# First pair of gate and up tiles as eight plain block products, and the second norm's roots in two steps

## The chip, the cores and the metric

The kernel runs on one core of one Trainium2 chip. The metric is the device time of one execution in microseconds (us), the median over several runs. Five engines work side by side and are ordered by semaphores: TensorE (PE, with its weight loads shown as PEld), VectorE (DVE), ScalarE (ACT), GpSimd (POOL) and SyncE (SP), which issues the DMAs.

## The reference

One layer of a decoder for 1024 prompt tokens and 8 x 8 sample tokens. What matters here is its second half; the input projection, the convolution heads and the attention come before it:

```python
x = x + jnp.concatenate([a, o], axis=-1) @ w_out          # output projection, residual
h = rms_norm(x, norm_ffn_g)                               # second norm, over 1024 features
g_full = jnp.concatenate([ffn_past, h @ w_ffn_gate], axis=1)
g = depthwise_conv_valid(g_full, ffn_conv_w, ffn_conv_b)  # width 3, along the tokens
x = x + (jax.nn.silu(g) * (h @ w_ffn_up)) @ w_ffn_down
```

with `rms_norm(x, g) = x * rsqrt(mean(x * x) + 1e-6) * g`. D_MODEL is 1024 and D_FF is 2816; everything is float32.

## The kernel before

Activations lie with features on the partitions: `x2` is 8 tiles (KT) of 128 features by N = 1088 tokens (1024 + 64). The tokens are taken in two halves of HN = 544. Each float32 operand is split into a high part, which ScalarE rounds to the fast matmul type, and a low part, the difference, which VectorE makes for activations (`split`) and POOL for weights (`weight_parts`). A product is then three matmuls: high by high, high by low, low by high. One block product is 4 feature tiles x 2 pieces of 272 tokens x 3 = 24 matmuls of 128x272.

The stage of this study ("F" in the code) does three things one after the other.

- `out_half(0)` and `out_half(1)`: the last part of the output projection, for the first and the second half of the tokens. For each of the 8 feature tiles it multiplies 12 matmuls, adds the result into `x2` (VectorE), stores the tile to DRAM (`x2d`, a DMA on SP's queue), squares it (ScalarE) and adds the square to a running sum (VectorE). 
- `rstd`: the norm's factor of one half. Matmuls with a column of ones add the sum up over the partitions and put the tokens on the partitions (L191), VectorE and ScalarE form 1/sqrt on a small tile (L193 to L206), and transposes (L213) and a copy spread it over all partitions again. For the first half this stands inside `out_half(1)`, behind its fourth tile (`norm_first`, m == 3); for the second half behind its last tile.
- `ffn_pair(j)` for j = 0 to 10: the gate's and up's tiles j and j + 11 (HF = 11). Two feature tiles of output, two halves of the input features and two halves of the tokens make a 2 x 2 block product, formed in Winograd's way with seven block products in place of eight (`products`). It needs sums and differences of token blocks (b11, b21 and b22 are plain blocks; t1 to t4 are combined) and of weight blocks (s1 to s4, made by `blocks_of_both` with four VectorE sums, L918 to L921).

The first pair differs: PE has nothing else to do while the blocks are being made. `products(..., first=True)` takes the seven products in another order (b11, b21, b22, t3, t2, t1, t4). `first_blocks` makes the b11 and b21 blocks of the first token half: four scales (`scale`, multiplying x by the norm's factor and weight), then four splits.

The order of the instructions on each engine comes from a scheduler, which takes them by a model of their times; `tc.issue_after(i)` adds an edge that keeps what is inside behind instruction i. Accumulators lie in four pairs of PSUM banks (`pair`: px, py, pz, pv).

## Time and profile before

| | |
|---|---|
| median of 3 runs | 1429.69 us (1428.96 to 1431.0) |
| profiled execution | 1432.72 us, span 1430.9 us |
| mean granted TensorE clock | 0.975 |
| busy, share of the span | PE 94%, PEld 89%, DVE 60%, ACT 36%, POOL 30% |
| stage F | 603.6 to about 1135 us of the span |
| instructions in stage F on PE | 192 matmuls of the output projection, 3696 of gate and up |

Times in the profile count from the start of the span. A row of the timeline gives start, duration, engine, line, operation, out<-in, count and, in brackets, the idle time ahead of it and what ended it. Busy shares are averages over stages with different limits. The matmuls overlap on PE, so a row of a matmul lasts longer than the distance to the next.

### The profile page before, as it was taken

The numbers are of one execution on the slowest core, as the hardware profiler recorded it, in microseconds if no ns is written. First come the engines' busy times: TensorE is split into PE (matmuls) and PEld (weight loads), VectorE is DVE, ScalarE is ACT, GpSimd is POOL, SyncE is SP. The second block draws the span as 40 slices with busy tenths as digits, with TensorE's granted clock in tenths as the row PEclk, the third lists the DMA queues.
The fourth block names the chain that finished last, engine by engine and source line by source line (L and its number), as shares of the span: only waits on it lengthen the run. The fifth ranks groups of instructions, "written<-read, shape, count | busy, mean of one in ns | idle before, by whom it ended". The sixth has DMA issues, their size and how long they took to land.

```text
span 1430.9 us, 24745 instructions
## 1 busy us (share of the span) xinstructions
PE 1350.0 (94%) x10011; PEld 1280.5 (89%) x10011; DVE 861.0 (60%) x1649; ACT 514.3 (36%) x982; POOL 431.5 (30%) x303
## 2 busy tenths in 40 slices
PE   6999999999999998976999999999999999999995
PEld 6988889999977777876899999999999889999995
DVE  7398595566574665679756566655656642423146
ACT  5312211457565564345333323333332321212033
POOL 3221111110000115231454445545445211224124
PEclk9999999999999998987999999999999999999998
DMA  7246676746699887340022122122212571414003
GB/s 271 54 139 245 226 255 206 206 141 179 180 276 226 243 228 225 112 162 8 30 91 91 65 87 91 52 70 91 91 62 91 167 291 45 139 48 131 11 9 118
DMA packets 84882, 195.16 MB, mean 136 GB/s; under 512 B 12576, under 2 KB 46752, under 8 KB 84768
## 3 DMA queue, kind: packets, MB, share of 16 engines
q1 hardware_dynamic: 84768, 193.57, 42.8%
q8 instruction: 79, 1.29, 0.4%
q14 instruction: 35, 0.29, 0.1%
HBM read 145.03 MB, written 48.52 MB: 135 GB/s over the span
## 4 chain that ended last, share of the span: by engine, by line
PE 76%; DVE 12%; DMA 6%; issue 2%; POOL 1%; ACT 1%; SPq 1%; POOLq 0%; ACTq 0%; DVEq 0%
PE g L174 9%; PE g L172 9%; PE g L173 9%; PE py L840 4%; PE py L842 4%; PE py L843 4%; DVE cacc L333 4%; PE o L666 3%; PE s L581 3%; PE pz L843 3%; PE pz L842 3%; PE pz L840 3%; PE px L843 3%; PE px L840 3%; PE px L842 3%; PE t L649 3%
## 5 line engine op out<-in xcount | busy, mean ns | idle before, releaser
L148 POOL TENSOR_TENSOR wl<-wr,wh 128x768 fp32r<-128x768 f32 (+2 forms) x61 | 117.1, 1921 | 464.7 <-PE g L174 391.8
L172 PE MATMUL g<-xh,wh 128*128 128x384 f32 (+1 forms) x472 | 158.6, 336 | 0.0
L173 PE MATMUL g<-xl,wh 128*128 128x384 f32 (+1 forms) x472 | 157.4, 333 | 0.0
L174 PE MATMUL g<-xh,wl 128*128 128x384 f32 (+1 forms) x472 | 157.2, 333 | 0.0
L172 PE MATMUL g<-ah,wh 128*128 128x384 f32 (+1 forms) x432 | 141.6, 333 | 5.0 <-ACT ah L1135 3.3
L173 PE MATMUL g<-al,wh 128*128 128x384 f32 (+1 forms) x432 | 143.0, 331 | 1.7 <-DVE al L1136 1.7
L174 PE MATMUL g<-ah,wl 128*128 128x384 f32 (+1 forms) x432 | 142.7, 331 | 0.7 <-POOL wl L148 0.7
L146 ACT ACTIVATE wh<-wr 128x768 fp32r<-128x768 f32 (+2 forms) x62 | 52.0, 838 | 241.0 <-PE g L174 177.5
L903 POOL TENSOR_TENSOR s<-wr,s 128x1024 fp32r<-128x1024 f32 x44 | 107.5, 2444 | 89.7 <-ACT s L902 47.9
L1158 DVE TENSOR_TENSOR x<-g,x 128x384 f32<-128x384 f32 (+1 forms) x72 | 38.0, 534 | 137.4 <-PE g L174 137.2
L622 ACT ACTIVATE y<-y,m 128x128 f32<-128x128 f32 (+1 forms) x192 | 88.4, 463 | 32.9 <-DVE m L610 32.9
L174 PEld LDWEIGHTS g<-xh,wl 128*128 128x128 f32 x472 | 90.0, 191 | 2.3 <-issue 2.1
L585 DVE CUSTOM_DVE_ANT_0 y<-s,pmk 128x128 f32<-128x128 f32 (+1 forms) x192 | 63.9, 378 | 45.8 <-PE s L581 36.9
L172 PEld LDWEIGHTS g<-xh,wh 128*128 128x128 f32 x472 | 90.1, 191 | 1.4 <-issue 1.2
L173 PEld LDWEIGHTS g<-xl,wh 128*128 128x128 f32 x472 | 90.0, 191 | 1.1 <-issue 1.0
L172 PEld LDWEIGHTS g<-ah,wh 128*128 128x128 f32 x432 | 82.0, 191 | 5.9 <-ACT ah L1135 3.6
L173 PEld LDWEIGHTS g<-al,wh 128*128 128x128 f32 x432 | 81.9, 190 | 2.0 <-DVE al L1136 2.0
L174 PEld LDWEIGHTS g<-ah,wl 128*128 128x128 f32 x432 | 81.8, 189 | 1.0 <-POOL wl L148 1.0
L333 DVE SCALAR_TENSOR_TENSOR cacc<-gp,prm,cacc 128x1024 f32<-128x1024 f32 x60 | 80.1, 1335 | 0.1
L1087 DVE SCALAR_TENSOR_TENSOR fc<-gb,prm,fc 128x1104 f32<-128x1104 f32 x44 | 79.0, 1813 | 2.0 <-ACT fc L1085 1.2
L903 POOL TENSOR_TENSOR wa<-wr,wa 128x1024 fp32r<-128x1024 f32 (+1 forms) x23 | 56.3, 2448 | 76.3 <-ACT wa L902 76.3
L381 DVE TENSOR_TENSOR qkv<-g,rb 128x384 f32<-128x384 f32 (+1 forms) x53 | 41.2, 777 | 46.0 <-PE g L174 45.9
(307 smaller groups left out, 4118.1 us busy)
## 6 DMA issues: line engine op xcount, KB each, us to landing
cr<-in_kc SPq DMA_DIRECT2D x24, 768.0 KB, 8.8
cr<-in_vc SPq DMA_DIRECT2D x24, 768.0 KB, 7.7
kk<-dk SPq DMA_DIRECT2D x48, 256.0 KB, 7.3
u<-u SPq DMA_DIRECT2D x22, 544.0 KB, 3.0
ur<-u SPq DMA_DIRECT2D x22, 544.0 KB, 4.8
wr<-in_w_in SPq DMA_DIRECT2D x22, 512.0 KB, 4.9
wr<-in_w_gate SPq DMA_DIRECT2D x22, 512.0 KB, 3.3
wr<-in_w_up SPq DMA_DIRECT2D x22, 512.0 KB, 4.5
```

What stands on the lines that cost most here:

```text
L148: lo_eng.tensor_sub(lo, raw, hi.bitcast(F32))
L172: nc.tensor.matmul(ps[c], whi[:, k, :], xh[:, t0:t0 + n], start=(k == 0), stop=False)
L173: nc.tensor.matmul(ps[c], whi[:, k, :], xl[:, t0:t0 + n], start=False, stop=False)
L174: nc.tensor.matmul(ps[c], wlo[:, k, :], xh[:, t0:t0 + n], start=False, stop=(k == nk - 1))
L333: eng.scalar_tensor_tensor(acc[:, :S], gp[:, j:j + S], col(w0 + j), acc[:, :S], op0=ALU.mult, op1=ALU.add)
L585: nc.vector.tensor_tensor_reduce(out=y[:, o:o + n], in0=ps[:, o:o + n], in1=mask, op0=ALU.add, op1=ALU.min, scale=1.0, scalar=3e38, accum_ ...
L622: nc.scalar.activation(y, y, AF.Exp, bias=m[:, 4 * g + i:4 * g + i + 1], scale=-1.0, accum_out=den[:, g, 2 * hd + u, i:i + 1])
L840: nc.tensor.matmul(ps, whi[:, k, :], xh[:, t], start=(start and k == 0), stop=False, skip_group_check=True)
L842: nc.tensor.matmul(ps, whi[:, k, :], xl[:, t], start=False, stop=False, skip_group_check=True)
L843: nc.tensor.matmul(ps, wlo[:, k, :], xh[:, t], start=False, stop=(k == nk - 1), skip_group_check=True)
L903: nc.gpsimd.tensor_sub(lo, x, hi.bitcast(F32))
L1087: nc.vector.scalar_tensor_tensor(c[:, :W], gb[i][:, t:t + W], col(C_FW + 3 * f + t), c[:, :W], op0=ALU.mult, op1=ALU.add)
```

## The change

1. `rstd` is cut into `root` (ones-matmuls and the small steps up to 1/sqrt) and `spread` (transposes and copy), with `sizes` for the pieces. The first half's root is now called behind tile 2 of `out_half(1)` (m == 1) and its spread behind tile 5 (m == 4). The second half's root is called between the first pair's b11 and b21 products, and its spread behind the second block of the b21 products (`spread_second`).
2. For the first pair, gate and up are eight plain block products each, in the order in which the blocks are made. `two_products` takes one block of tokens and two weight blocks, one feature tile after the other, and adds to two accumulators. `first_half` does b11 and b21 (the copies `shared`, taken after b11, and `kept`, after b21, go to SBUF on ScalarE); `second_half` does b22 and t1 (t1 is the second token half less the first, so that the b11 result in `shared` is used again). The gate's and up's first halves come one after the other, then the gate's second half, then up's.
3. The first pair needs no s1 to s4, so its four weight sums and the splits of the sums are gone for gate and up, and raw weights are split instead. t2, t3 and t4 serve the other ten pairs alone and are made later; t4 in two parts behind up's second half.
4. In `first_blocks` a scale and a split alternate, and the scales wait for the low part made two blocks earlier.

The products of the other ten pairs stay as they are. PE gets 8638 rows for 8590 (a row is a piece of the recorded order, most of them one matmul), DVE 1598 for 1599, ACT 694 for 692, POOL 304 for 308.

```diff
@@ -179,14 +179,15 @@
-        rooted = [None]
-        def rstd(sq, div, new, width=N):
+        def sizes(width):
+            return [min(P, width - i) for i in range(0, width, P)]
+        def root(sq, div, width):
             ps = bank(*rbank[0])
-            nt = -(-width // P)
-            size = [min(P, width - i * P) for i in range(nt)]
+            size = sizes(width)
+            nt = len(size)
             for i, n in enumerate(size):
@@ -203,7 +204,12 @@
             nc.vector.scalar_tensor_tensor(t, t, -0.5, v, op0=ALU.mult, op1=ALU.mult)
-            rooted[0] = nc.vector.scalar_tensor_tensor(r, t, 1.5, r, op0=ALU.add, op1=ALU.mult).ins
+            nc.vector.scalar_tensor_tensor(r, t, 1.5, r, op0=ALU.add, op1=ALU.mult)
+            return r
+        def spread(r, new, width):
+            size = sizes(width)
             rb = new("rb")
@@ -214,6 +220,9 @@
             return rb
+        def rstd(sq, div, new, width=N):
+            return spread(root(sq, div, width), new, width)
@@ -843,6 +852,23 @@
+        def two_products(outs, ws, x, start, hook=lambda k, last: None):
+            n = HN // 2
+            nk = len(x)
+            for k, (xh, xl) in enumerate(x):
+                for o, (whi, wlo) in zip(outs, ws):
+                    for c in range(2):
+                        ps = o[:, PO:512] if c == 0 else o[:, 512:PO + HN]
+                        t = slice(c * n, c * n + n)
+                        nc.tensor.matmul(ps, whi[:, k, :], xh[:, t], start=(start and k == 0), stop=False,
+                                         skip_group_check=True)
+                        nc.tensor.matmul(ps, whi[:, k, :], xl[:, t], start=False, stop=False, skip_group_check=True)
+                        last = nc.tensor.matmul(ps, wlo[:, k, :], xh[:, t], start=False, stop=(k == nk - 1),
+                                                skip_group_check=True).ins
+                hook(k, last)
         def all_of(ps):
@@ -876,11 +902,12 @@
         blocks = {tag: [None] * 4 for tag in BTAGS}
+        made = []
...
             nc.scalar.activation(hi, x, AF.Copy)
-            nc.vector.tensor_sub(lo, x, hi.bitcast(F32))
+            made.append(nc.vector.tensor_sub(lo, x, hi.bitcast(F32)).ins)
             blocks[tag][k] = hi, lo
@@ -927,12 +954,15 @@
-        first_gate = weight_blocks(w_gate, 0)
-        first_up = weight_raw(w_up, 0)
-        first_up_a = []
+        raw = weight_raw(w_gate, 0)
+        gate0 = blocks_of_first(raw) + weight_parts(raw[1], [wp.tile([P, D], F32R, tag="W", name=nm("wa"))
+                                                             for _ in range(2)])
+        raw = weight_raw(w_up, 0)
+        up0 = []
         for i in range(2):
-            x = first_up[0][:, i * half:i * half + half]
-            first_up_a += weight_parts(x, [slot("t4", "wa", w=half) for _ in range(2)])
+            up0 += weight_parts(raw[0][:, i * half:i * half + half], [slot("t4", "wa", w=half) for _ in range(2)])
+        up0 += weight_parts(raw[1], [wp.tile([P, D], F32R, tag="W", name=nm("wa")) for _ in range(2)])
@@ -960,53 +990,89 @@
-        def norm_half(sq):
-            return rstd(sq, D, lambda s: slot("t3", s, F32), HN)
+        def new_root(s):
+            return slot("t3", s, F32)
         sq0, _ = out_half(0, lambda *_: None)
-        r0 = []
+        rs = []
         def norm_first(m, added):
-            if m == 3:
-                r0.append(norm_half(sq0))
+            if m == 1:
+                rs.append(root(sq0, D, HN))
+            elif m == 4:
+                rs[0] = spread(rs[0], new_root, HN)
...
             for i in range(k, k + 4):
-                with tc.issue_after(after):
-                    scale(0, i, r0[0])
-            for i in range(k, k + 4):
+                with tc.issue_after(made[-2] if len(made) > 1 else after):
+                    scale(0, i, rs[0])
                 with tc.issue_after(after):
...
         sq1, added = out_half(1, norm_first)
-        r1 = norm_half(sq1)
+        quads = [(*halves(x2[k]), *halves(x2[k + 4])) for k in range(4)]
+        def first_half(w, between=lambda: None, hook=lambda k, last: None):
+            a11, a12, a21, a22 = w
+            o = pair("px"), pair("py")
+            two_products(o, (a11, a21), blocks["b11"], True)
+            shared = [zt("F", "tmp", 4, "ta", HN) for _ in o]
+            for t, ps in zip(shared, o):
+                nc.scalar.activation(t, all_of(ps), AF.Copy)
+            between()
+            two_products(o, (a12, a22), blocks["b21"], False, hook)
+            kept = [slot("t4", "c1", F32) for _ in o]
+            for t, ps in zip(kept, o):
+                nc.scalar.activation(t, all_of(ps), AF.Copy)
+            return kept, shared
+        def second_half(w):
+            a11, a12, a21, a22 = w
+            o = pair("pv"), pair("pz")
+            two_products(o, (a12, a22), blocks["b22"], True)
+            two_products(o, (a11, a21), blocks["t1"], False)
+            return o
+        def between():
+            rs.append(root(sq1, D, HN))
+            first_blocks(4, "b21", added)
+        def spread_second(k, last):
+            if k == 1:
+                with tc.issue_after(last):
+                    rs[1] = spread(rs[1], new_root, HN)
         first_blocks(0, "b11", added)
-        first_blocks(4, "b21", rooted[0])
+        g1, g_shared = first_half(gate0, between, spread_second)
+        r1 = rs[1]
         for k in range(4):
...
             split(x2[k + 4][:, HN:], "b22", k)
-        quads = [(*halves(x2[k]), *halves(x2[k + 4])) for k in range(4)]
+        u1, u_shared = first_half(up0)
         for k, (x11, x12, x21, x22) in enumerate(quads):
...
             nc.vector.tensor_sub(x11, x12, x11)
+            split(x11, "t1", k)
+        g2 = second_half(gate0)
+        for k, (x11, x12, x21, x22) in enumerate(quads):
             nc.vector.tensor_sub(x12, x22, x12)
             split(x12, "t3", k)
-        for k, (x11, x12, x21, x22) in enumerate(quads):
             nc.vector.tensor_sub(x22, x22, x11)
             split(x22, "t2", k)
-        for k, (x11, x12, x21, x22) in enumerate(quads):
-            split(x11, "t1", k)
-        for k, (x11, x12, x21, x22) in enumerate(quads):
-            nc.vector.tensor_sub(x21, x21, x22)
-            split(x21, "t4", k)
+        def last_blocks(ks):
+            for k in ks:
+                x11, x12, x21, x22 = quads[k]
+                nc.vector.tensor_sub(x21, x21, x22)
+                split(x21, "t4", k)
...
-        def products(weights, c11, put, first=False):
+        def products(weights, c11, put):
...
@@ -1075,19 +1122,27 @@
-            products(weight_blocks(w_gate, j) if j else first_gate, c11, put, j == 0)
+            if j:
+                products(weight_blocks(w_gate, j), c11, put)
+            else:
+                for i in range(2):
+                    nc.scalar.activation(gb[i][:, 2:2 + HN], g1[i], AF.Copy)
+                    put(i, 1, g2[i], g_shared[i])
             cv = []
...
                 nc.gpsimd.tensor_copy(cfo[:, f, 2:18].rearrange("p (b t) -> p b t", t=2), past(gb[i])[:, :, T:T + 2])
-                c = keep("fc", GW)
+                c = (keep if i or j else spare)("fc", GW)
                 nc.scalar.activation(c[:, :W], gb[i][:, 0:W], AF.Identity, bias=col(C_FB + f), scale=col(C_FW + 3 * f))
...
                 cv.append(c)
+            if j == 0:
+                last = second_half(up0)
+                last_blocks((0, 1))
             u = [(spare if j else keep)("u") for _ in range(2)]
@@ -1108,7 +1163,15 @@
-            products(weight_blocks(w_up, j) if j else first_up_a + blocks_of_both(first_up), u11, put_u)
+            if j:
+                products(weight_blocks(w_up, j), u11, put_u)
+                return
+            for i in range(2):
+                nc.vector.tensor_mul(u[i][:, :HN], u1[i], cv[i][:, :HN])
+                nc.vector.tensor_add(u[i][:, HN:N], all_of(last[i]), u_shared[i])
+                times(i, HN, N)
+                nc.sync.dma_start(ud[i * HF], u[i])
+            last_blocks((2, 3))
```

The diff moves line numbers: L191 and L213 of before are L192 and L219, a scale is L991 for L961, a low part L910 for L883, a sum of squares L985 for L955, a store of `x2d` L979 for L949.

The order of the two programs at the three places that matter. First PE around the two roots, before (`g` is an accumulator of the output projection or of a root, `mh`/`ml` and `wh`/`wl` are the split operands, `sq` the sum of squares, `rr` the factor, `px` and `py` accumulators of the first pair):

```order
L843 MATMUL g_6897<-mh_6634,wl_6645 128x272
L191 MATMUL g_1278_6915<-ones,sq_6716 128x1 x4
L191 MATMUL g_1278_6915<-ones,sq_6716 32x1
L213 MATMUL g_1283_6933<-ident,rr_6925 128x128 x4
L213 MATMUL g_1284_6939<-ident,rr_6925 128x32
L840 MATMUL g_6942<-mh_6628,wh_6650 128x272
...
L843 MATMUL g_6996<-mh_6634,wl_6655 128x272
L191 MATMUL g_1293_7014<-ones,sq_6859 128x1 x4
L191 MATMUL g_1293_7014<-ones,sq_6859 32x1
L213 MATMUL g_1298_7032<-ident,rr_7024 128x128 x4
L213 MATMUL g_1299_7038<-ident,rr_7024 128x32
L840 MATMUL px_7216<-b11h_7045,wa_6662 128x272
L842 MATMUL px_7216<-b11l_7046,wa_6662 128x272
```

Half 0's root stands behind four tiles of half 1, the second root behind the eighth, and the first pair behind that. And after the change:

```order
L852 MATMUL g_6854<-mh_6634,wl_6641 128x272
L192 MATMUL g_1273_6872<-ones,sq_6709 128x1 x4
L192 MATMUL g_1273_6872<-ones,sq_6709 32x1
L849 MATMUL g_6889<-mh_6628,wh_6644 128x272
...
L852 MATMUL g_6925<-mh_6634,wl_6651 128x272
L219 MATMUL g_1284_6944<-ident,rr_6882 128x128 x4
L219 MATMUL g_1285_6950<-ident,rr_6882 128x32
L849 MATMUL g_6953<-mh_6628,wh_6650 128x272
...
L852 MATMUL g_6989<-mh_6634,wl_6655 128x272
L865 MATMUL px_7027<-b11h_7008,wa_6662 128x272
L865 MATMUL py_7028<-b11h_7008,wa_6666 128x272
L192 MATMUL g_1304_7081<-ones,sq_6852 128x1 x4
L192 MATMUL g_1304_7081<-ones,sq_6852 32x1
L867 MATMUL px_7027<-b11l_7009,wa_6662 128x272
```

The first root's ones stand behind two tiles, its transposes behind five, and the second root's ones between the first matmuls of the b11 products.

VectorE where the b11 blocks are made, before (`x_...` are the tiles of `x2`, `rb` the spread factor, `b11h` and `b11l` the parts of a block):

```order
L955 TENSOR_TENSOR sq_6859<-sq_7011,sq_6859 128x544
L961 SCALAR_TENSOR_TENSOR x_1099_5934<-x_1099_5934,prm,rb_6932 128x544
L961 SCALAR_TENSOR_TENSOR x_1106_5974<-x_1106_5974,prm,rb_6932 128x544
L961 SCALAR_TENSOR_TENSOR x_1113_6014<-x_1113_6014,prm,rb_6932 128x544
L961 SCALAR_TENSOR_TENSOR x_1120_6054<-x_1120_6054,prm,rb_6932 128x544
L195 TENSOR_SCALAR rv_7020<-g_1293_7014 128x4
L198 TENSOR_SCALAR rv_7020<-g_1293_7014 32x1
L883 TENSOR_TENSOR b11l_7046<-x_1099_5934,b11h_7045 128x544
L883 TENSOR_TENSOR b11l_7050<-x_1106_5974,b11h_7049 128x544
L883 TENSOR_TENSOR b11l_7054<-x_1113_6014,b11h_7053 128x544
L200 RECIPROCAL rr_7024<-rv_7020 128x5
L883 TENSOR_TENSOR b11l_7058<-x_1120_6054,b11h_7057 128x544
```

Four scales came first and the low parts after them. After the change:

```order
L985 TENSOR_TENSOR sq_6852<-sq_7004,sq_6852 128x544
L991 SCALAR_TENSOR_TENSOR x_1099_5934<-x_1099_5934,prm,rb_6943 128x544
L991 SCALAR_TENSOR_TENSOR x_1106_5974<-x_1106_5974,prm,rb_6943 128x544
L910 TENSOR_TENSOR b11l_7009<-x_1099_5934,b11h_7008 128x544
L991 SCALAR_TENSOR_TENSOR x_1113_6014<-x_1113_6014,prm,rb_6943 128x544
L910 TENSOR_TENSOR b11l_7014<-x_1106_5974,b11h_7013 128x544
L991 SCALAR_TENSOR_TENSOR x_1120_6054<-x_1120_6054,prm,rb_6943 128x544
L910 TENSOR_TENSOR b11l_7019<-x_1113_6014,b11h_7018 128x544
L991 SCALAR_TENSOR_TENSOR x_1127_6094<-x_1127_6094,prm,rb_6943 128x544
L196 TENSOR_SCALAR rv_7087<-g_1304_7081 128x4
L199 TENSOR_SCALAR rv_7087<-g_1304_7081 32x1
L910 TENSOR_TENSOR b11l_7024<-x_1120_6054,b11h_7023 128x544
```

Scales and low parts alternate, and scales of b21 stand ahead of the last low part of b11; the second root's steps stand among them.

SP's queue where up's first raw weights (`wr`) are loaded, before and, in the second fence, after:

```order
L949 DMA x2d_6693<-x_1099_5934 128x544
L949 DMA x2d_6694<-x_1106_5974 128x544
L949 DMA x2d_6695<-x_1113_6014 128x544
L949 DMA x2d_6696<-x_1120_6054 128x544
L896 DMA wr_6681<-in_w_up 128x1024
L896 DMA wr_6683<-in_w_up 128x1024
L949 DMA x2d_6697<-x_1127_6094 128x544
L949 DMA x2d_6698<-x_1134_6134 128x544
```

```order
L979 DMA x2d_6690<-x_1127_6094 128x544
L923 DMA wr_6670<-in_w_up 128x1024
L979 DMA x2d_6691<-x_1134_6134 128x544
L923 DMA wr_6672<-in_w_up 128x1024
L979 DMA x2d_6692<-x_1141_6174 128x544
L979 DMA x2d_6693<-x_1148_6214 128x544
L979 DMA x2d_6686<-x_1099_5934 128x544
L923 DMA wr_7655<-in_w_gate 128x1024
```

Before, up's loads stood behind four stores of half 1; now they stand among the last stores of half 0, and the second pair's gate loads begin behind the first store of half 1.

More of the change, by code (lines that the diff above doesn't have):

```diff
@@ L1016, in products @@
             nc.scalar.activation(ta, all_of(x), AF.Copy)
-            if first:
-                block_product(x, a12, blocks["b21"], False)
-                c11(x)
-                v, z, y = pair("pv"), pair("pz"), pair("py")
-                block_product(v, s4, blocks["b22"], True)
-                block_product(z, s3, blocks["t3"], True)
-                block_product(y, s2, blocks["t2"], True)
-                put(1, 0, y, ta)
-                block_product(y, s1, blocks["t1"], False)
-                nc.vector.tensor_add(tb, all_of(y), ta)
-                put(0, 1, v, tb)
-                put(1, 1, z, tb)
-            else:
-                y, z = pair("py"), pair("pz")
-                block_product(y, s2, blocks["t2"], True)
-                put(1, 0, y, ta)
-                block_product(x, a12, blocks["b21"], False)
-                c11(x)
-                block_product(y, s1, blocks["t1"], False)
-                nc.vector.tensor_add(tb, all_of(y), ta)
-                block_product(z, s3, blocks["t3"], True)
-                put(1, 1, z, tb)
-                block_product(y, s4, blocks["b22"], False)
-                put(0, 1, y, ta)
+            y, z = pair("py"), pair("pz")
+            block_product(y, s2, blocks["t2"], True)
+            put(1, 0, y, ta)
+            block_product(x, a12, blocks["b21"], False)
+            c11(x)
+            block_product(y, s1, blocks["t1"], False)
+            nc.vector.tensor_add(tb, all_of(y), ta)
+            block_product(z, s3, blocks["t3"], True)
+            put(1, 1, z, tb)
+            block_product(y, s4, blocks["b22"], False)
+            put(0, 1, y, ta)
             block_product(z, a22, blocks["t4"], False)
@@ L1060, in c11 @@
             def c11(ps):
[L1061 to L1067 removed]
+                nc.scalar.activation(gb[0][:, 2:2 + HN], all_of(ps), AF.Copy)
             def put(i, h, ps, x):
```

7 lines of the change are left out of this document (removed).

## The prediction

> **What bounds the kernel now.** I first read the busy shares and then the span cut at the places where the program changes stage. The page's first part and the table of windows (window, its length, then busy time and count for PE, PEld, DVE, ACT and POOL, then granted clock, DMA share and GB/s) give:
>
> ```profile
> span 1430.9 us, 24745 instructions
> PE 1350.0 (94%) x10011; PEld 1280.5 (89%) x10011; DVE 861.0 (60%) x1649; ACT 514.3 (36%) x982; POOL 431.5 (30%) x303
> ...
> 603.60:624.40 20.80, 18.55 (x145) 18.16 (x144) 19.05 (x29) 10.80 (x19) 4.19 (x2) 1.00 0.47 170
> 624.40:652.20 27.80, 13.51 (x79) 12.30 (x78) 21.46 (x39) 12.99 (x22) 7.65 (x4) 0.69 0.30 110
> 652.20:684.00 31.80, 24.64 (x145) 23.02 (x144) 31.75 (x50) 16.20 (x27) 10.79 (x4) 0.84 0.00 1
> 684.00:726.00 42.00, 38.41 (x294) 36.98 (x294) 25.84 (x31) 15.53 (x17) 20.87 (x19) 1.00 0.22 78
> 726.00:1120.00 394.00, 394.00 (x3153) 394.00 (x3152) 243.18 (x273) 131.43 (x141) 195.81 (x152) 1.00 0.23 77
> 1120.00:1135.00 15.00, 14.18 (x113) 13.90 (x112) 10.53 (x11) 5.01 (x6) 4.09 (x2) 1.00 0.46 139
> ```
>
> The fifth window is the yardstick: TensorE never stops, one matmul of 128x272 every 394.00/3153 = 0.125 us. The whole stage (output projection of the two halves, then eleven pairs of gate and up) is 192 + 11 x 2 x 7 x 24 = 3888 such matmuls, 486.0 us at that pace, and lasts 531.4 us. So 45.4 us are lost, 0.9 of them in the last window and none in the fifth: **44.5 us are lost between 603.6 and 726**, exactly where the change works. There TensorE isn't the bound. In 624.40:652.20 it is busy for half the time, and in 652.20:684.00 VectorE is busy for 31.75 of 31.80 us. What PE waits for there (total, times, longest):
>
> ```profile
> PE g L213 <- DVE rv L193: 5.8, 1, 5.8
> PE g L213 <- DVE rr L206: 4.4, 1, 4.4
> PE g L191 <- DVE sq L955: 4.1, 2, 2.4
> PE py L840 <- ACT t2h L882: 4.1, 1, 4.1
> PE px L842 <- DVE b21l L883: 2.0, 1, 2.0
> ```
>
> These are the two roots (ones-matmul L191, vector steps, transposes L213) and the blocks of the Winograd form. The waits are fewer than 44.5 us because the slow clock and short gaps make up the rest. The rows around the first root, and one cold stretch:
>
> ```profile
> L903 POOL TENSOR_TENSOR s<-wr,s 128x1024 fp32r<-128x1024 f32 x44 | 107.5, 2444 | 89.7 <-ACT s L902 47.9
> ...
> 624.23 0.29 PE L843 MATMUL g<-mh,wl 128*128 128x272 f32 x1
> 626.25 1.18 PE L191 MATMUL g<-ones,sq 128*128 128x1 f32 x10 [1.73 <-DVE sq L955]
> 633.24 1.33 PE L213 MATMUL g<-ident,rr 128*128 128x128 f32 x5 [5.81 <-DVE rv L193]
> ...
> 660.49 0.40 PE L842 MATMUL px<-b21l,wa 128*128 128x272 f32 x1 [1.98 <-DVE b21l L883]
> 662.70 0.43 PE L842 MATMUL px<-b21l,wa 128*128 128x272 f32 x1
> ...
> 672.62 0.51 PE L840 MATMUL py<-t2h,s 128*128 128x272 f32 x1 [4.05 <-ACT t2h L882]
> 672.93 0.43 PE L840 MATMUL px<-b11h,wa 128*128 128x272 f32 x1
> 676.10 0.32 PE L843 MATMUL px<-b11h,wa 128*128 128x272 f32 x1
> ...
> 617.92 0.68 DVE L918 TENSOR_TENSOR wr<-wr 128x512 f32<-128x512 f32 x1
> 625.40 0.71 DVE L955 TENSOR_TENSOR sq<-sq,sq 128x544 f32<-128x544 f32 x1
> 626.66 2.34 DVE L955 TENSOR_TENSOR sq<-sq,sq 128x544 f32<-128x544 f32 x1
> 629.11 2.67 DVE L955 TENSOR_TENSOR sq<-sq,sq 128x544 f32<-128x544 f32 x1
> 632.92 0.17 DVE L206 SCALAR_TENSOR_TENSOR rr<-rt,rr 128x5 f32<-128x5 f32 x1
> ...
> 626.07 5.14 POOL L903 TENSOR_TENSOR s<-wr,s 128x1024 fp32r<-128x1024 f32 x2 [9.91 <-ACT s L902]
> 673.25 10.76 POOL L1058 COPY gb<-sft 128x16 f32<-128x16 f32 x1
> ```
>
> Three things are to be seen. After a gap of 4.05 us the fourteen matmuls from 672.93 to 676.10 come every 0.226 us, so a gap of that length costs about 15 x 0.101 = 1.5 us more; the row of 662.70 shows the slow pace even behind a gap of 1.98. The sums of squares (L955) take 0.71 us alone, but 2.34 and 2.67 beside POOL's two splits of 626.07: the root's short vector steps stood in line behind them, and the chain from ones to rr took until 633.09. And POOL's small copy took 10.76 us beside a VectorE that never paused.
>
> **The change part by part.**
>
> *More matmuls.* Gate and up of the first pair take 8 products each for 7: 2 x 24 = 48 more matmuls, 48 x 0.125 = **+6.0 us**, all on PE's path.
>
> *The first root, earlier.* The first window's loss, 20.80 - 145 x 0.125 = 2.7 us, comes before the change and stays. The order has the ones-matmuls 24 matmuls (3.0 us) earlier, so PE reaches them near 624.4 - 3.0 = 621.4. The sum they read was ready at 626.1 (row 625.40). The four weight sums L918 to L921, about 0.6 us each (row 617.92), leave VectorE's queue ahead of it, but one step of it stood beside other SBUF work and POOL's splits now come earlier, so I take only 0.7 of these 2.4 us: ready at 625.45. PE waits **4.05 us**, and the ones take **1.2** (row 626.25). From their end (627.43) to rr's (633.09) it was 5.7 us, of which 2.34 + 2.67 - 2 x 0.71 = 3.6 went to the two long sums; the short steps now stand together, with one sum ahead of them. The 2.1 that are left and 0.85 for that sum and the square root's table put rr at 629.6. PE meanwhile has 36 matmuls (tiles 2 to 4 of half 1; 4.5 us, to 632.9 with the cold stretch) and no longer waits for rr: the 5.8 us of that wait go. The gap ahead of the ones brings a cold stretch, 1.5 us by the row and 0.25 for a clock that comes back later: **1.75**. The transposes then run warm in about **0.7** (half of the row's 1.33 at the slow clock), and tiles 5 to 7 end at 638.2.
>
> *From the last tile to the first product.* The rows that stand here before:
>
> ```profile
> 637.62 0.72 DVE L948 TENSOR_TENSOR x<-g,x 128x544 f32<-128x544 f32 x1 [4.52 <-PE g L843]
> 639.13 0.72 DVE L955 TENSOR_TENSOR sq<-sq,sq 128x544 f32<-128x544 f32 x1 [0.78 <-ACT sq L951]
> 644.73 2.87 DVE L961 SCALAR_TENSOR_TENSOR x<-x,prm,rb 128x544 f32<-128x544 f32 x4
> 645.54 2.75 ACT L882 ACTIVATE b11h<-x 128x544 fp32r<-128x544 f32 x4 [1.50 <-DVE x L961]
> 647.65 1.97 DVE L883 TENSOR_TENSOR b11l<-x,b11h 128x544 fp32r<-128x544 f32 x3
> ...
> 644.96 1.60 PE L191 MATMUL g<-ones,sq 128*128 128x1 f32 x10 [2.37 <-DVE sq L955]
> 650.95 1.33 PE L213 MATMUL g<-ident,rr 128*128 128x128 f32 x5 [4.38 <-DVE rr L206]
> 657.75 0.40 PE L840 MATMUL px<-b21h,wa 128*128 128x272 f32 x1 [0.59 <-ACT ta L1016]
> ```
>
> Residual add, square and sum of one tile take 637.62 to 639.85, 2.2 us; after 638.2 the sum of half 1 is ready at 640.5. A scale is 0.72 and the high part follows 0.8 after its start (644.73 to 645.54), taking 0.66: the first b11 block is there at about 642, and PE waits **3.8 us**. It then goes cold again, **1.5**. Before, the first product began at 652.2, after the second root had run with PE idle (waits of 2.4 and 4.4). Now the second root's ones (**1.6**) stand between the first b11 matmuls, its vector steps between the splits, and its transposes (**0.7**) behind the second block of b21, with matmuls on either side. The b11 blocks come one per 1.3 us (a scale and a split), each feeding 12 matmuls, 1.5 us warm: PE just stays behind them. The copies of the b11 result make the b21 products wait **0.55** (the row of 657.75).
>
> *The blocks after.* VectorE needs a scale and a low part for each of four b22 blocks and a scale, a difference and a low part for each of four t1: 20 operations at 0.635 apart = 12.7 us behind b21. b21's products end near 658.3, up's first half near 670.3. I get the last b22 low part at 666.4, needed from 670.3 on, and the last t1 at 674.0, needed from 676.3: covered by 2 to 4 us. If the cover goes, the excess comes on PE one for one. t2, t3 and t4 are needed only by the second pair, at 694 and later. The wait of 4.1 us for t2h goes, and nothing takes its place. The eight weight sums of the first pair and four splits vanish from VectorE and POOL; both were off PE's path apart from the first root, so they earn nothing more.
>
> *Loads and the second pair.* The loads of a raw weight tile, and POOL's narrow splits (x2):
>
> ```profile
> 635.64 2.52 POOL L903 TENSOR_TENSOR wa<-wr,wa 128x512 fp32r<-128x512 f32 x2 [4.44 <-ACT wa L902]
> ...
> wr<-in_w_gate SPq DMA_DIRECT2D x22, 512.0 KB, 3.3
> wr<-in_w_up SPq DMA_DIRECT2D x22, 512.0 KB, 4.5
> ```
>
> Up's second load is now issued ahead of the last stores of half 0, and the second pair's gate loads ahead of most stores of half 1. Their weight chain (split on ACT and POOL, four sums, two wide splits of 2.44 us each on POOL, from the grouped row above) must be ready at 697. By my count its last wide split ends at 696.3 to 700, and I add **1.5 us** of stall for it. The copies of the two first halves to SBUF (0.6 us each) are on ACT, which was busy for 16.20 of 31.80 us at the most, and but for the 0.55 above cost nothing. The new ta and c1 take no DMA.
>
> *The sum.* Lost after: 2.7 + 4.05 + 1.2 + 1.75 + 0.7 + 3.8 + 1.5 + 1.6 + 0.7 + 0.55 + 1.5 = 20.05 us in place of 44.5. Gain 24.45 - 6.0 = 18.4 us. The profiled execution took 1432.7 us, 3.0 above the median 1429.69; taken from the median, 1429.7 - 18.4 = **1411.3 us**.
>
> *Bounds of what the trace doesn't show.* The wait of 4.05 us can be zero (sum ready as PE arrives), and the two cold stretches, 3.25 us together, can stay away: 7.3 us less, near 1404; with the 1.5 of the second pair gone too, 1403. On the other side, a lockout such as POOL's 10.76 us row can hit the weight chain or the blocks: up to 10 us more, 1421.
>
> **A page against the change.** On this page PEld is busy for 89% of the span, more than VectorE's 60%. The Trainium skill, "Perfetto Trace Analysis", section "Identifying the Most-Contended Engine", judges TensorE's headroom by the share in which weights are loaded, and would have the most loaded engine relieved first. By it 48 more matmuls with their weight loads cost 6.0 us whatever the other engines do. The windows disagree for this stage: PEld has 12.30 of 27.80 us and 23.02 of 31.80.
>
> **Rivals.**
> 1. *No cover, only more matmuls.* The waits move elsewhere and the 6.0 us stand: 1435.7. For it speaks the 89% of weight loads over the whole span, against it that PE idles for 14 of 27.8 us in one window of this very stage. Chance 2 in 100.
> 2. *Slower: the second pair's gate load blocks VectorE's queue.* That load takes the buffer of an earlier raw tile, which POOL's split (2.44 us) frees at about 627.75 by my count, and the sums L945 on its data stand in VectorE's queue ahead of the last sums of half 1. A load that lands 3.3 to 4.5 us later is there by 632, and L945's turn comes at 634.5: 2.5 us of slack, then every us goes straight to the end. The kernel turns slower if the POOL split ends more than 2.5 + 18.4 = 21 us late. The copy of 10.76 us shows that POOL can be shut out for 11 us, not for 21. 1430 to 1440; chance 4.
> 3. *Smaller gain: VectorE stays the bound.* It was full in 652.20:684.00, and needs as long for scales and blocks as before; if the b22 and t1 blocks are also held up by POOL's splits (2.34 for 0.71), PE waits 8 to 10 us in second half and second pair: 1419 to 1421. Chance 18.
> 4. *Larger gain.* The sum is ready when PE arrives and the clock stays up: 1403 to 1406. For it speaks that the weight sums (L918) leave VectorE's queue whole, 2.4 us and not 0.7; against it that a gap of 1.98 was enough for the slow clock. Chance 14.
>
> My forecast, 1407 to 1418, has 62. The range 1403 to 1421 leaves out rivals 1 and 2 and the outer part of rivals 3 and 4, which are less sharp than their numbers: some 14 to 20 in 100. A difference under 0.2% (2.9 us) can't be told from none here: faster 0.92 (the forecast, rival 4 and all but a rest of rival 3), the same 0.03 (that rest and a part of rival 2), slower 0.05 (rivals 1 and 2).
>
> **What would show it.** In the new trace: ones of half 0 at about 625.5 after a wait of some 4 us; the first px matmul at 642 rather than 652; no wait for t2h; transposes without a wait; 48 more matmuls in the stage, and the pace of 0.125 from about 700 on. A wait for s, wa or w22 weights (L930) of over 3 us, or for b22l and t1l, would put me too low; no cold rows would put me too high. If PE waits as long for sq at 634 as it did for rr, rival 2 is it.

## The result and the profile after

The changed kernel took 1421.69 us (median of 9 runs, 1416.23 to 1429.17), the kernel before 1430.95 us beside it (9 runs): a ratio of **0.9948**, 95% interval 0.993 to 0.9965. It is faster by 0.5%, some 7 us by the ratio (the two medians lie 9.3 us apart), where 18.4 were forecast, and it lies just past the upper end of the range (1421).

Single executions of one kernel differ by 10 us and more, and the profile shows where: the stage of the output projection and of gate and up (stage F) begins at 605.09 us in the profiled execution before, at 597.50 after, and between 595 and 611 in the other kernels below, although the traces hold the same instructions ahead of it, TensorE's in the same order. So 7.6 of the 14.2 us between the two spans (1430.9 and 1416.7) are such drift, and I compare **stage F itself**, from its first output-projection matmul to its last matmul, counted from start to start, with one matmul's 0.125 us added for the last. First and last rows of it, before and then after (start and duration in us, engine, line, operation, out<-in, shapes):

```profile
605.09 0.77 PE L840 MATMUL g<-mh,wh 128*128 128x272 f32 x4 [1.43 <-ACT mh L862]
...
1134.62 0.29 PE L843 MATMUL pz<-t4h,w 128*128 128x272 f32 x1
```

```profile
597.50 0.77 PE L849 MATMUL g<-mh,wh 128*128 128x272 f32 x4 [1.43 <-ACT mh L888]
...
1121.27 0.28 PE L852 MATMUL pz<-t4h,w 128*128 128x272 f32 x1
```

Stage F took 529.7 us before and 523.9 after: 5.8 us less, which agrees with the interval of the ratio (5.0 to 10.0 us). The windows of the prediction, moved by 7.6 us so that they begin at the same work, in the changed kernel:

```profile
core 0: us, PE busy (x) PEld busy (x) DVE busy (x) ACT busy (x) POOL busy (x), PEclk, DMA share, GB/s
596.01:616.81 20.80, 15.62 (x121) 15.12 (x120) 19.09 (x26) 13.44 (x22) 8.70 (x4) 1.00 0.64 222
616.81:644.61 27.80, 23.21 (x138) 22.75 (x139) 24.37 (x43) 12.43 (x21) 4.13 (x3) 0.75 0.33 109
644.61:676.41 31.80, 31.80 (x253) 31.40 (x252) 25.68 (x43) 17.39 (x31) 7.67 (x2) 1.00 0.01 1
676.41:718.41 42.00, 41.31 (x330) 41.09 (x329) 33.19 (x38) 19.18 (x21) 24.71 (x24) 1.00 0.20 66
718.41:1112.41 394.00, 387.66 (x3059) 383.45 (x3058) 237.43 (x265) 124.50 (x136) 198.83 (x143) 1.00 0.23 80
```

The windows two and three did what was forecast: 138 matmuls for 79, 253 for 145. The surprise is the last row. In the same 394 us, in which nothing was meant to change, TensorE issued 3059 matmuls where it had issued 3153. **94 matmuls, 11.8 us, were given back by the other ten pairs** (the window spans nine of them and a part). The waits of PE in stage F say on what:

```profile
PE py L852 <- POOL s L930: 4.6, 10, 0.7
PE px L865 <- DVE x L991: 3.8, 1, 3.8
PE g L192 <- DVE sq L985: 3.7, 1, 3.7
PE py L849 <- DVE u L1158: 2.4, 10, 0.3
```

Two waits come ten times each, once in every pair: t2's third matmul waits for `s`, the low part of a weight block from POOL, and t1's first waits until VectorE has read the accumulator `py` (`u`). From pair to pair it is 43.26 us, where it was 42.02.

The product of one such pair that waits, in the changed kernel:

```profile
790.51 0.63 ACT L929 ACTIVATE w<-wr 128x512 fp32r<-128x512 f32 x1 [4.18 <-PE pz L851]
794.60 0.65 DVE L1122 TENSOR_TENSOR gb<-py,ta 128x480 f32<-128x480 f32 x1
795.30 0.68 DVE L948 TENSOR_TENSOR wr<-wr 128x512 f32<-128x512 f32 x1
795.48 1.31 ACT L1137 ACTIVATE fc<-gb,prm 128x1104 f32<-128x1104 f32 x1 [4.34 <-DVE gb L1123]
796.70 1.99 ACT L929 ACTIVATE s<-wr 128x1024 fp32r<-128x1024 f32 x2
797.82 2.64 POOL L930 TENSOR_TENSOR s<-wr,s 128x1024 fp32r<-128x1024 f32 x1 [1.66 <-ACT s L929]
...
799.78 0.29 PE L851 MATMUL pz<-t3l,s 128*128 128x272 f32 x1
800.51 0.39 PE L852 MATMUL py<-t2h,s 128*128 128x272 f32 x1 [0.44 <-POOL s L930]
...
806.62 0.29 PE L851 MATMUL pz<-t3l,s 128*128 128x272 f32 x1
807.14 0.39 PE L849 MATMUL py<-t1h,s 128*128 128x272 f32 x1 [0.23 <-DVE u L1158]
...
798.75 7.71 DVE L1139 SCALAR_TENSOR_TENSOR fc<-gb,prm,fc 128x1104 f32<-128x1104 f32 x3
806.37 0.72 DVE L1158 TENSOR_TENSOR u<-py,ta 128x544 f32<-128x544 f32 x1
```

The same place before:

```profile
770.63 0.63 ACT L902 ACTIVATE w<-wr 128x512 fp32r<-128x512 f32 x1 [4.43 <-PE py L842]
774.85 0.69 DVE L921 TENSOR_TENSOR wr<-wr 128x512 f32<-128x512 f32 x1
775.57 2.21 ACT L902 ACTIVATE s<-wr 128x1024 fp32r<-128x1024 f32 x2 [1.22 <-DVE wr L921]
776.71 2.42 POOL L903 TENSOR_TENSOR s<-wr,s 128x1024 fp32r<-128x1024 f32 x1 [3.29 <-PE py L843]
...
782.15 0.29 PE L843 MATMUL py<-t2h,s 128*128 128x272 f32 x1
...
788.77 0.28 PE L840 MATMUL py<-t1h,s 128*128 128x272 f32 x1
...
780.38 7.12 DVE L1087 SCALAR_TENSOR_TENSOR fc<-gb,prm,fc 128x1104 f32<-128x1104 f32 x4
787.41 0.72 DVE L1103 TENSOR_TENSOR u<-py,ta 128x544 f32<-128x544 f32 x1
```

Slack is the time between an operand's being ready and its being wanted. Before, s's low part was ready at 779.13 and wanted at 782.15: 3.0 us of slack. To see what became of it, count both from the first row, the split of the product's last raw weights (`w`), which starts when TensorE is done with the t1 (before) or t3 (after) of the product ahead; the weight sums, s's high part and POOL's low part follow from it.

- t2's third matmul was wanted 11.5 us after that row before and 9.4 after (799.91, right behind the row of 799.78). Fewer matmuls stand between: 17, or 2.1 us, because t2 no longer waits behind 19 matmuls of b21.
- The low part was ready 8.5 us after that row before and 9.95 after (800.46). VectorE now makes `gb` from py ahead of its last weight sum (794.60), and ScalarE does a step of the convolution (`fc`) ahead of s's high part, so POOL's split starts 1.2 us later; and it takes 2.64 us for 2.42.

Together that is 3.6 us against 3.0 of slack. Likewise `u`: before, VectorE had read py at 788.13 and t1 wanted it at 788.77, 0.6 us of slack; after, it had read it at 807.09 and t1 was due at 806.75. Of this 1.0 us, half is again TensorE's order (27 matmuls for 31 between t2 and t1) and half VectorE's reading, which stands behind the convolution. In matmuls per group, TensorE's order in this product is (b22 and t4 belong to the product begun earlier, the 2 of b11 ahead of t1 to the next):

```
before   b11 24 | b22 24, t4 24 | t2 2, b21 19, t2 22, b21 5 | t3 24, b11 2 | t1 24
after    b11 8 | b22 24, t4 24 | b11 16 | t2 2, t3 2, t2 22 | b21 24 | t3 3, t1 24, t3 19
```

No line of the diff is about these orders, TensorE's, VectorE's and ScalarE's. They come from the scheduler.

### The profile page after: what moved, and what is told of

Same layout as the page of the kernel before. It is cut to its first block, busy times and chain, and to the rows that moved or that the text cites. A ratio compares the mean times of both kernels' runs of the same rounds, so it can differ in the third digit from the quotient of the medians.

```text
span 1416.7 us, 24825 instructions
## 1 busy us (share of the span) xinstructions
PE 1351.9 (95%) x10059; PEld 1280.7 (90%) x10059; DVE 853.0 (60%) x1636; ACT 512.1 (36%) x984; POOL 436.5 (31%) x299
## 4 chain that ended last, share of the span: by engine, by line
PE 74%; DVE 13%; DMA 4%; issue 3%; POOL 3%; ACT 1%; SPq 1%; POOLq 0%; DVEq 0%; ACTq 0%
PE g L172 10%; PE g L174 10%; PE g L173 10%; DVE cacc L342 4%; PE py L852 4%; PE py L849 4%; PE py L851 4%; PE o L675 3%; PE s L590 3%; PE t L658 3%; PE px L849 2%; PE px L852 2%; PE px L851 2%; PE pz L849 2%; PE pz L852 2%
## 5 line engine op out<-in xcount | busy, mean ns | idle before, releaser
L930 POOL TENSOR_TENSOR s<-wr,s 128x1024 fp32r<-128x1024 f32 x40 | 117.5, 2958 | 65.4 <-ACT s L929 62.8
L1139 DVE SCALAR_TENSOR_TENSOR fc<-gb,prm,fc 128x1104 f32<-128x1104 f32 x44 | 97.8, 2243 | 8.8 <-ACT fc L1137 8.5
L174 PEld LDWEIGHTS g<-xh,wl 128*128 128x128 f32 x472 | 89.1, 189 | 2.0 <-issue 1.8
L930 POOL TENSOR_TENSOR wa<-wr,wa 128x1024 fp32r<-128x1024 f32 (+1 forms) x25 | 59.6, 2389 | 91.3 <-ACT wa L929 87.5
```

The costliest lines, as they stand in the source:

```text
L174: nc.tensor.matmul(ps[c], wlo[:, k, :], xh[:, t0:t0 + n], start=False, stop=(k == nk - 1))
L930: nc.gpsimd.tensor_sub(lo, x, hi.bitcast(F32))
L1139: nc.vector.scalar_tensor_tensor(c[:, :W], gb[i][:, t:t + W], col(C_FW + 3 * f + t), c[:, :W], op0=ALU.mult, op1=ALU.add)
```

## The experiments

Each kernel's stage F in its own profiled execution, the distance from pair to pair (from one gate's first b22 matmul to the next), the slow matmuls (those of 128x272 that last 0.42 us or more, in the first 140 us of the stage, each counted singly, also where the timeline merges two into one row; each costs about 0.1 us more than the others), and the ratio to the kernel before with its interval:

| kernel | pair, us | stage F, us | slow matmuls | ratio |
|---|---|---|---|---|
| before | 42.02 | 529.7 | 59 | 1 |
| changed | 43.26 | 523.9 | 37 | 0.9948 (0.993 to 0.9965) |
| e1 b21 first | 42.97 | 524.1 | 59 | 0.9927 (0.990 to 0.9954) |
| e2 t2 first, in before | 43.23 | 551.5 | 103 | 1.012 (1.0091 to 1.015) |
| e3 root only | 42.02 | 527.8 | 80 | 0.9979 (0.9954 to 1.0003) |
| e4 plain products only | 43.25 | 526.5 | 44 | 0.9942 (0.9919 to 0.9965) |
| e5 old order | 42.00 | 512.5 | 25 | 0.9893 (0.9856 to 0.993) |
| e6 narrow low part | 42.08 | 513.4 | 54 | 0.9859 (0.9816 to 0.9903) |
| e7 late weight sums | 42.00 | 515.3 | 54 | 0.9855 (0.9822 to 0.9889) |
| e8 later root | 42.00 | 511.8 | 31 | 0.9843 (0.9816 to 0.987) |
| e9 later root, narrow | 42.08 | 508.8 | 21 | 0.9849 (0.9821 to 0.9878) |

The slow matmuls alone move a stage by about 3 us, so a difference of that size between two single stages says little. In e1, e2, e3, e4, e6 and e8, 13 to 15 of them (1.4 us) stand in the first 6 us of the stage, ahead of everything that the edits change; the other kernels have none there. The distance from pair to pair is steady to 0.05 us in the steady pairs of one kernel and says most.

### e1: b21 ahead of t2

```diff
-            block_product(y, s2, blocks["t2"], True)
-            put(1, 0, y, ta)
             block_product(x, a12, blocks["b21"], False)
             c11(x)
+            block_product(y, s2, blocks["t2"], True)
+            put(1, 0, y, ta)
```

> The changed kernel, but in the ten other pairs b21's product is written ahead of t2's, which puts it there on TensorE too. Theory A (the order of the ten other pairs on TensorE costs the shortfall: t2's matmuls now start before POOL's low part s and before VectorE has read py): the waits for s (4.6 us in all) and for u (2.4 us) vanish, the distance from pair to pair falls from 43.26 to 42.0 us, and the stage from its first output-projection matmul to the last t4 matmul falls from 523.9 to about 512 us; time about 0.9845 of before. Rival B (POOL's s split takes 2.8 to 3.5 us in place of 2.4 because VectorE's sums and convolution now fall beside it, whatever TensorE does): the wait for s only moves to another product, the distance stays at 43 us or more and the time at 0.993 to 0.997 of before.

The waits in the window from 760 to 1120 us:

```profile
PE py L849 <- DVE u L1158: 5.4, 8, 0.7
PE px L852 <- POOL wa L930: 0.9, 1, 0.9
```

A miss for theory A as I had it, and not what rival B said either, though rival B's numbers nearly came. The wait for s is gone, so s is on time once b21 stands ahead of t2. But t1 now follows t2 with 22 matmuls of t3 between (2.75 us) in one product of each pair, and waits 0.68 us for VectorE's reading of py. 42.97 us a pair, nothing gained in the stage. 22 more slow matmuls (2.2 us) stand against what the pairs gained.

### e2: the changed kernel's order in the kernel before

```diff
-                block_product(y, s2, blocks["t2"], True)
+                last = block_product(y, s2, blocks["t2"], True)
                 put(1, 0, y, ta)
-                block_product(x, a12, blocks["b21"], False)
+                with tc.issue_after(last):
+                    block_product(x, a12, blocks["b21"], False)
```

`block_product` returns its last matmul here. The order that came out on TensorE in the other pairs is group for group the one of the changed kernel.

> The kernel before with one edge in products: in the ten other pairs b21's product stays behind t2's. Nothing of the first pair and of the roots is changed. Theory A: the distance from pair to pair grows from 42.02 to about 43.26 us with waits for s and u in each, stage 529.8 -> about 542 us, time 1.008 of before. Rival B (the pairs are slow because the first pair's new order leaves VectorE, ScalarE and POOL in another phase): 42.0 us a pair, time 1.000 of before within 0.002.

Its waits from 760 to 1120 us:

```profile
PE py L843 <- POOL s L904: 3.5, 8, 0.5
PE py L840 <- DVE u L1105: 1.9, 8, 0.2
```

The same two waits of the same size, 43.23 us a pair, and 1.2% slower. With the first pair in Winograd's form and the root in one step, one edge on TensorE is enough to bring the loss: theory A. But the edge moved more than TensorE. VectorE and ScalarE came out in the changed kernel's order too, with `gb` made from py ahead of the last weight sum and `fc` ahead of s's high part. So the order of the pairs as a whole is shown to be the cause, and not TensorE's share of it alone. The stage grew by 21.8 us, more than the 12 us expected: besides the pairs the edges cost some 10 us at the first two pairs, where t2 waited 2.6 and 1.3 us for s's high part, and 44 more matmuls were slow.

### e3 and e4: the two halves of the change

e3 is the kernel before with the first root in two steps; e4 is the changed kernel without that:

```diff
 def norm_first(m, added):       # e3
-    if m == 3:
-        r0.append(norm_half(sq0))
+    if m == 1:
+        r0.append(root(sq0, D, HN))
+    elif m == 4:
+        r0[0] = spread(r0[0], lambda s: slot("t3", s, F32), HN)
```

```diff
 def norm_first(m, added):       # e4
-    if m == 1:
-        rs.append(root(sq0, D, HN))
-    elif m == 4:
-        rs[0] = spread(rs[0], new_root, HN)
+    if m == 3:
+        rs.append(rstd(sq0, D, new_root, HN))
```

> The kernel before with only the first half's root in two steps (root behind tile 2, spread behind tile 5 of half 1); first pair in Winograd's form as before. Theory A: the pairs stay at 42.02 us. The wait of 5.8 us for rr at the first transposes goes, one of about 3.7 us ahead of the ones comes (1.7 before), one cold stretch stays: stage 529.8 -> about 525.5 us, time 0.997 of before. Rival (the root was hidden by the second root's wait that follows, and the time only moves there): 529 to 530 us, 1.000.

> The changed kernel, with the first half's root whole again behind tile 4 of half 1. Theory A: the pairs stay at 43.26 us, since the plain products bring the other order; the front is 4 us longer than in the changed kernel: stage about 528 us, time 0.998 of before. Rival (the two-step root brings the other order): 42.0 us a pair, stage about 516 us, 0.990.

The roots' rows of e3:

```profile
624.63 1.32 PE L192 MATMUL g<-ones,sq 128*128 128x1 f32 x10 [4.12 <-DVE sq L963]
631.79 0.77 PE L218 MATMUL g<-ident,rr 128*128 128x128 f32 x5
640.49 1.21 PE L192 MATMUL g<-ones,sq 128*128 128x1 f32 x10 [2.68 <-DVE sq L963]
646.57 1.32 PE L218 MATMUL g<-ident,rr 128*128 128x128 f32 x5 [4.87 <-DVE rr L207]
```

The 5.8 us ahead of the first transposes are gone, and 4.12 ahead of the ones have taken the place of 1.73. Stage F gains 1.9 us of the 4 expected, with 21 slow matmuls more (2.1 us), 14 of them at the stage's start. The ratio's interval holds 1. In e4 the wait stands at the transposes again:

```profile
619.09 1.18 PE L192 MATMUL g<-ones,sq 128*128 128x1 f32 x10 [0.67 <-DVE sq L985]
625.39 1.33 PE L219 MATMUL g<-ident,rr 128*128 128x128 f32 x5 [5.12 <-DVE rv L194]
```

and stage F is 2.6 us longer than the changed kernel's, 13 slow matmuls (1.3 us) at its start included. So by the stage the two-step root is worth 1.9 and 2.6 us, 3.3 and 1.3 without the slow matmuls at the start; the times don't show it, since e3's interval holds 1 and e4's ratio is no higher than the changed kernel's. What is clear is that the other order comes with the plain products alone: 42.02 us a pair in e3, 43.25 in e4.

### e5: the other pairs put back into their old order

```diff
-            block_product(y, s2, blocks["t2"], True)
+            b21 = block_matmuls(x, a12, blocks["b21"], False)
+            last = run(b21[:19])
+            last = run(block_matmuls(y, s2, blocks["t2"], True), last)
             put(1, 0, y, ta)
-            block_product(x, a12, blocks["b21"], False)
+            last = run(b21[19:], last) if b21[19:] else last
             c11(x)
-            block_product(y, s1, blocks["t1"], False)
+            last = run(block_matmuls(z, s3, blocks["t3"], True), last)
+            run(block_matmuls(y, s1, blocks["t1"], False), last)
             nc.vector.tensor_add(tb, all_of(y), ta)
-            block_product(z, s3, blocks["t3"], True)
             put(1, 1, z, tb)
```

`block_matmuls` lists the matmuls of a block product and `run` issues them behind `last`; both are new in this kernel and left out here.

> The changed kernel with the ten other pairs put by edges into the order that they had before on TensorE: 19 matmuls of b21, t2, the other 5 of b21, t3, and only then t1. e1 showed that b21 ahead of t2 alone trades the wait for s (0.44 us a pair) for one for u (0.68), since t1 then follows t2 at 22 matmuls' distance. Theory A (each pair needs both: s later than POOL's split, t1 later than VectorE's reading of py): no wait for s or u, 42.02 us a pair, stage 524 -> 512 us, time 0.984 to 0.988 of before. Rival B (VectorE's and POOL's own order is what is slow): one of the two waits stays, 42.5 to 43.2 us a pair, 0.992.

The window 760 to 1100 us, before, after and in e5:

```profile
760.00:1100.00 340.00, 340.00 (x2721) 340.00 (x2720) 210.42 (x233) 111.59 (x120) 168.41 (x129) 1.00 0.24 80
```

```profile
760.00:1100.00 340.00, 335.02 (x2648) 331.70 (x2647) 202.57 (x230) 105.25 (x116) 172.24 (x127) 1.00 0.22 75
```

```profile
760.00:1100.00 340.00, 340.00 (x2722) 340.00 (x2722) 209.29 (x236) 114.03 (x123) 170.92 (x132) 1.00 0.22 77
```

No wait in the steady pairs, 42.00 us each, stage F 512.5 us: within 1.2 us of the 511.3 that the prediction's gain would have left (529.7 - 18.4). That it is so close is partly luck: 12 fewer slow matmuls than in the changed kernel gain 1.2 us, and the edges bring a wait of 1.8 us for `ta` in the second pair. VectorE and ScalarE went back to their old order along with TensorE, so e5 doesn't separate the engines either. Busy times can't show the difference well, since rows of matmuls overlap: PE reads 335.02 in the changed kernel for 340.00 before, although 73 matmuls (9.1 us) fewer were issued.

### e6: POOL's low part in two pieces

```diff
-            s2, s4 = weight_parts(g, [wide("s24") for _ in range(2)])
+            hi, lo = [wide("s24") for _ in range(2)]
+            nc.scalar.activation(hi, g, AF.Copy)
+            for i in range(2):
+                t = slice(i * half, i * half + half)
+                nc.gpsimd.tensor_sub(lo[:, t], g[:, t], hi[:, t].bitcast(F32))
```

(Then s2 and s4 are cut from hi and lo as in `weight_parts`.)

> The changed kernel, with POOL's low part of s2 and s4 made as two subtractions of 128x512 in place of one of 128x1024, in all ten other pairs; TensorE's order in them stays t2 ahead of b21. Theory A (t2 waits for POOL's wide split alone): s2's low part is there some 1.2 us earlier, the wait of 0.44 and its slow start go (0.6 us a pair), the wait for u of 0.24 stays: 42.6 to 42.7 us a pair, stage 523.9 -> 518 us. Rival B (s is late because POOL starts late, not because its split is wide): wait stays, 43.2 us a pair.

The first piece in a product of the kind that had waited, t2's third matmul, and the next split:

```profile
852.58 1.53 POOL L953 TENSOR_TENSOR s<-wr,s 128x512 fp32r<-128x512 f32 x1 [1.66 <-ACT s L950]
854.67 0.29 PE L852 MATMUL py<-t2h,s 128*128 128x272 f32 x1
856.39 3.46 POOL L930 TENSOR_TENSOR s<-wr,s 128x1024 fp32r<-128x1024 f32 x1
```

42.08 us a pair, better than the 42.6 to 42.7 expected. t2 still stands ahead of b21, and VectorE and ScalarE keep the changed kernel's order in this product; t2 needs only the first piece, ready at 854.11, and the wait for s is gone without any edge. The wait for u went too. The reason is visible in the order: in this product 12 and no longer 3 matmuls of t3 stand ahead of t1. VectorE had read py at 861.66 and t1 started at 861.93; 9 matmuls fewer would have had it due at 860.8. (The other product of a pair didn't wait in the changed kernel.) The wide split still takes 3.46 us, so that slowness by itself costs nothing; what waits for it decides.

### e7: the second pair's weight sums later

In e5's kernel the first of the four sums stands in `with tc.issue_after(made[7])`, behind b21's last low part, and the others follow it.

> e5's kernel, with the weight sums of the second pair's gate (two of them stood on VectorE ahead of the last sums of squares of half 1) held behind b21's last low part. Theory A: the first product starts 1.2 us earlier (38.1 -> 36.9 us after the stage's start) and the wait for its block falls from 3.8 to 2.6 us; stage another 1.2 us shorter than e5's, about 511 us. Rival: the second pair's weights come later for it and t2 of the second pair waits for s as long: no gain against e5.

A miss. In e5 the first product already began 36.8 us after the stage's start (38.1 in the changed kernel), so there was little left to take: 36.5 us, and a wait of 3.7 for 4.0. Stage F was 2.8 us longer than e5's, and 29 more slow matmuls are 2.9 us. 14 of them follow the wait of 1.8 us for `ta` in the second pair, which e5 has too, without a slow stretch behind it. The ratio, 0.9855, overlaps e5's. Nothing is shown either way.

### e8 and e9: the first root later

The changed kernel waits 3.7 us ahead of the ones. e8 is e5, e9 is e6, with the root moved:

```diff
-            if m == 1:
+            if m == 3:
                 rs.append(root(sq0, D, HN))
-            elif m == 4:
+            elif m == 6:
                 rs[0] = spread(rs[0], new_root, HN)
```

> e5's kernel (plain products, the other pairs in their old order) with the first half's root behind tile 4 and its spread behind tile 7 of half 1, in place of 2 and 5. Theory A (PE stands 3.7 us ahead of the ones because it gets there before the sum of half 0 is ready, and goes to the slow clock after it): the wait falls to about 0.7 us, there is no slow stretch behind it (12 to 21 matmuls at 0.1 us each in the runs before), the transposes still wait for nothing, and half 1 ends 3 to 5 us earlier; pairs 42.0 us; stage 512.5 -> 508 to 510 us. Rival (the first block waits for VectorE's scales and the root, whenever half 1 ends): the 3 us come back as a longer wait ahead of the first product (4.0 -> 7 us), stage 512 to 513 us.

> e6's kernel (POOL's low part of s2 and s4 in two pieces, no edges on the pairs) with the same later root and spread as e8. Theory A: 42.1 us a pair, stage 513.4 -> 509 to 511 us, time 0.982 to 0.986 of before. Rival: as for e8, 513 us.

PE's rows of e8:

```profile
616.89 1.18 PE L192 MATMUL g<-ones,sq 128*128 128x1 f32 x10 [0.78 <-DVE sq L1007]
631.68 0.60 PE L887 MATMUL px<-b11h,wa 128*128 128x272 f32 x1 [6.00 <-ACT b11h L931]
```

The wait ahead of the ones fell from 3.7 to 0.78 us and the one ahead of the first product grew from 4.0 to 6.0: 2.0 of the 2.9 came back there, as the rival said. The slow stretch behind the ones is gone, as theory A said. Stage F moved by 0.7 us, but e8 has 14 slow matmuls (1.4 us) at the stage's start that e5 lacks. In e9 it moved by 4.6, of which 33 fewer slow matmuls are 3.3; 14 of them stood at e6's start. Setting aside those at the start, the later root is worth 2.1 us in e8, between theory and rival, and 3.2 in e9, as theory A had it. The times can't show it: both kernels beat the changed one clearly, 0.984 and 0.985 of before, but against e5 and e6 their intervals overlap.

## Why the prediction was wrong, by its own steps

**The step that failed** is in its last lines and in no term of its sum: "the pace of 0.125 from about 700 on". The forecast put what the other ten pairs lose at nothing, with no reason beyond their products staying as they are, but for 1.5 us in the second pair (where one wait of 0.7 us for s came). They lost 1.24 us each. From the first product of the second pair to the stage's end it was 432.8 us, for 420.0 us of matmuls: 12.8 us lost where the forecast had 2.4 (its 1.5 and the last window's 0.9). e2, e4 and e5 show the cause: the order of the instructions there, which came with the plain products, costs it in either kernel, and the old order gives it back. e6 shows through what: with s's low part there earlier and t1 later, the new order costs next to nothing (42.08). What the scheduler found in the plain products to choose it, was not tried, and TensorE's order wasn't separated from VectorE's and ScalarE's. The slack could have been read from the trace before, 3.0 us for s and 0.6 for u, and the new order from the two programs.

**The front was right to 2 us.** From the stage's first matmul to the second pair's first product it took 91.1 us, for 89.1 forecast (the sum's first window starts 1.5 us ahead of that matmul). Term by term, forecast and then measured: the wait ahead of the ones 4.05, 3.71; the ones 1.2, 1.97 (at the slow clock); slow stretch 1.75, 21 matmuls or 2.1; transposes 0.7, 0.77; wait ahead of the first product 3.8, 3.81; slow stretch 1.5, 16 matmuls or 1.6; the second ones 1.6, 1.89; the second transposes 0.7, 0.77; the copy 0.55, no wait shown. These make 0.8 of the 2.0 us; the rest lies in gaps too short for this list. The two long waits have these rows:

```profile
617.59 1.97 PE L192 MATMUL g<-ones,sq 128*128 128x1 f32 x10 [3.71 <-DVE sq L985]
635.62 0.59 PE L865 MATMUL px<-b11h,wa 128*128 128x272 f32 x1 [3.81 <-DVE x L991]
```

No wait for t2h, b22l or t1l is left: the slack of 2 to 4 us held. The 48 more matmuls (6.0 us) were paid in full: PE had work throughout 644.61:676.41, where 253 matmuls at 0.125 us are 31.6 of 31.80 us.

**The rivals.** The smaller gain (rival 3, 1419 to 1421 us) named nearly the time that came, but by luck: its mechanism, late b22 and t1 blocks in the first pair, didn't happen. What took its place was outside the place that I had looked at. Rival 2's weight sums did stand ahead of the last sums of squares, but cost nothing to speak of: without them there (e7) the first product came 0.3 us earlier.

**The page on the most-contended engine.** The Trainium skill, "Perfetto Trace Analysis", section "Identifying the Most-Contended Engine", read over the whole span, would have had 6.0 us lost by the 48 more weight loads. e5 shows stage F 17.2 us shorter with those 48 in it, so a share over the whole span doesn't decide for one stage; in the steady pairs, where weight loads fill the window (340.00 of 340.00 us), the page's reading fits.

## What to carry to other kernels

Where a scheduler orders the instructions, compare the order over the whole program, the parts not meant to change first of all: a steady loop repeats a small loss, and here ten times 1.24 us took back two thirds of the gain. Ask for each accumulator and operand how much slack the old order gave it (3.0 and 0.6 us here), for that is what a new order spends. A loop's order that is known to be good is worth holding by edges, or its tightest hand-over worth splitting, before the code ahead of it is changed.

## What the runs showed of the hardware

In these rows POOL and VectorE shut each other out, and the one that came second paid. The kernel before, a wide split and a product on VectorE:

```profile
758.81 2.45 POOL L903 TENSOR_TENSOR s<-wr,s 128x1024 fp32r<-128x1024 f32 x1 [0.46 <-PE pz L843]
759.67 2.67 DVE L1094 TENSOR_TENSOR u<-u,fc 128x1024 f32<-128x1024 f32 x1
```

The same two in e6, where VectorE's started 0.02 us ahead:

```profile
833.21 1.23 DVE L1155 TENSOR_TENSOR u<-u,fc 128x1024 f32<-128x1024 f32 x1
833.23 3.46 POOL L930 TENSOR_TENSOR s<-wr,s 128x1024 fp32r<-128x1024 f32 x1
```

VectorE's product took 2.67 us behind POOL's split and 1.23 ahead of it; POOL's split took 2.45 ahead and 3.46 behind. The Trainium skill, "SBUF — State Buffer", section "Who interferes with whom", says so: a vector operation with two inputs in SBUF contends with a GpSimd instruction that reads SBUF, and the order of issue decides who waits. The rows agree.

The start of stage F moved between 595 and 611 us from execution to execution, with the same code ahead of it. A profile of one execution against one of another would have shown 14.2 us of gain here, where the runs show some 7.
